# P7 of the last five output blocks as seven inner products, with a hand-written order of four engines, in a pooling-mixer kernel

## The chip, the cores and the metric

The kernel runs on one core of one Trainium2 chip. The metric is device microseconds of one execution; lower is better. The names used for the engines are those of the profile: PE is TensorE's matrix multiplication and PEld its weight load, DVE is VectorE, ACT is ScalarE, POOL is GpSimd, SP is SyncE, which only issues transfers.

## The reference

With DEPTH = 1 only mixer 0 of the model is used. It works on x of 4096 rows and 1024 columns, in f32:

```python
normed = rms_norm(x, norm_w)
u, gate = split(normed @ in_w, 2)                 # in_w: 1024 x 2048
for g, window in enumerate((2, 4, 8, 16)):        # four groups of 256 channels
    pooled = trailing_mean(u[g], window) - u[g]
    mixed[g] = pooled @ group_w[g] + group_b[g]
y = mixed * scale * silu(gate)
h = x + y @ out_w                                 # out_w: 1024 x 1024
out = rms_norm(h, final_norm_w)
```

rms_norm divides each row by the root of the mean of its squares (plus 1e-6) and multiplies by a weight for each column. trailing_mean takes the mean of the last 2, 4, 8 or 16 rows.

## The kernel before

**Arithmetic.** TensorE multiplies in a reduced format (fp32r), so each f32 operand is split into a high half and a low half: `split` (L177) has ACT copy the high half and DVE subtract it from the source to get the low one. Each product is three passes, high x high, high x low and low x high (`mm3`, L774). Around that lies Strassen's scheme in Winograd's form: a multiplication of two matrices, each cut into 2 x 2 quarters, is made as seven products P1 to P7 of sums of quarters, instead of eight.

**Stages.** The group maps are folded into in_w on the chip first. The input stage takes four blocks of 1024 tokens, each for two halves of the channels, and stores y to DRAM (`yd`). The output stage, which this case is about, takes eight blocks of 512 tokens (`NBO = 8`, b = 0 to 7 in the code). For each it makes `y @ out_w` as P1, P7, P6, P2, P5, P4, P3 in this order (`ORDER_OUT`), adds x, and normalizes and stores the rows.

**One block of the output stage.** Quarters "11", "21", "12" and "22" of y are loaded (`load_o`, L1068) and each product's left operand is formed on DVE and split (`split_o`, L1082) into one of four operand tiles. The sums of Winograd's scheme are S1 = 21 + 22, S2 = S1 - 11, S3 = 11 - 21 and S4 = 12 - S2; S1 is P5's operand, S2 is P6's, S3 is P7's and S4 is P3's. The right operands, the seven sums of out_w, lie split in `w[P1]` to `w[P7]`. A product (`product_out`, L894) is 24 matmuls of 128 x 512: two halves of the rows (j), four slices of the inner dimension (k), three passes. They accumulate in PSUM banks; each block has four pairs of banks, x (P1, P2), v (P7, P4), y (P6, P5, P3) and a spare, and the pairs rotate from block to block (`sets_of`, L1315). ACT copies P1's result from x to y, so that P6, P5 and P3 accumulate on it, as P2 does on x.

`evict_o` (L1214) takes the results out. In the first seven blocks P7, P6 and P2 are copied by ACT into the row tiles `hs`, and a transfer on POOL's queue adds x to them in place (`add_h`, L1059); P5, P4 and P3 are added to them by DVE. In the last block x is loaded first (`load_h`, L1048) and all six are added by DVE. After P4 the lower rows are complete, after P3 the upper ones; `finish` (L1116) then has ACT square them (a full row tile of 1024 into an SBUF tile, with the sum alongside), POOL and DVE work out the reciprocal root (`inverse`, `rsqrt`), DVE scale the rows, and SP's queue store them. The last block's rows are finished in halves (`early_half`, `late_factor` L1163, `late_scalar`, `late_vector`).

**Inner products that exist already.** From the third block on P2 is itself made by Winograd's scheme: `split_inner` (L847) forms the left operands from the four quarters of "12" and their sums, `form_inner` (L819) the right ones once, in the second block, into four tiles that are kept, and `product_inner` (L867) is one inner product, six matmuls of 128 x 256. P2's seven are spread: five in P2's place, P6 inside P5, and two groups' results added to rows by DVE (`add_inner`, L884). In the input stage `product_seven` (L713) does the same for P7 of two blocks, with copies from one PSUM cell to another on ACT.

**Order.** The program is written step by step (product by product), and each step says how far ahead it may load (four steps) and split (two steps): `advance`, L1538. The order of the instructions on each engine is that of a scheduler, which works from the dependences and from hints of the form "issue this after that" (`tc.issue_after`). In the output stage there are few such hints.

Of the kernel before, what the change touches and what calls it, by code (L numbers as in the profile page):

```python
# [10 lines left out]
F32 = mybir.dt.float32  # L11
# [16 lines left out]
NV = 8  # L28
EPS = 1e-6
# [6 lines left out]
class Slots:  # L36
# [21 lines left out]
    def give(self, ap):  # L58
        _, t = self.used.pop(id(ap))
        Slots.clock += 1  # L60
        self.free.append((Slots.clock, t))


@with_exitstack
def kernel(
# [35 lines left out]
    nc = tc.nc  # L101

# [62 lines left out]
    def add(dst, a, b):  # L165
        nc.vector.tensor_tensor(out=dst, in0=a, in1=b, op=ALU.add)

    def sub(dst, a, b):
        return nc.vector.tensor_tensor(out=dst, in0=a, in1=b, op=ALU.subtract)  # L169

    def mul(dst, a, b):
        nc.vector.tensor_tensor(out=dst, in0=a, in1=b, op=ALU.mult)  # L172

    def copy(dst, src, func=AF.Copy):
        return nc.scalar.activation(dst, src, func)  # L175
# [32 lines left out]
    nc.vector.memset(eps, EPS)  # L208
    scrap = const.tile([P, 1], F32, name="scrap")
    nc.scalar.activation(scrap, eps, AF.Sqrt)  # L210
# [3 lines left out]
    def rsqrt(dst, tmp, ms, ss, on_vector=False, first=False):  # L214

        root = nc.scalar.activation(tmp, ss, AF.Sqrt, bias=eps, scale=1.0 / D).ins
        (nc.vector if on_vector and not first else nc.gpsimd).tensor_scalar(
            out=ms, in0=ss, scalar1=1.0 / D, scalar2=EPS, op0=ALU.mult, op1=ALU.add
        )
        nc.vector.reciprocal(out=dst, in_=tmp)  # L220
        if on_vector:
            mul(tmp, dst, ms)
            mul(tmp, tmp, dst)
            nc.vector.tensor_scalar(
                out=tmp, in0=tmp, scalar1=-0.5, scalar2=1.5, op0=ALU.mult, op1=ALU.add
            )
            done = nc.vector.tensor_tensor(out=dst, in0=dst, in1=tmp, op=ALU.mult).ins
            roots.append((root, done))
            return
        nc.gpsimd.tensor_tensor(out=tmp, in0=dst, in1=ms, op=ALU.mult)  # L230
        nc.gpsimd.tensor_tensor(out=tmp, in0=tmp, in1=dst, op=ALU.mult)
        nc.gpsimd.tensor_scalar(
            out=tmp, in0=tmp, scalar1=-0.5, scalar2=1.5, op0=ALU.mult, op1=ALU.add
        )
        nc.gpsimd.tensor_tensor(out=dst, in0=dst, in1=tmp, op=ALU.mult)  # L235
# [3 lines left out]
    def load_rows(mat, k, c):  # L239
        u = take()  # L240
        nc.sync.dma_start(
# [4 lines left out]
    def copy_scaled(dst, u, c):  # L246
        done = nc.scalar.activation(dst[:, 0], u, AF.Copy, scale=c)
        nc.vector.scalar_tensor_tensor(
# [5 lines left out]
    def scale_rows(u, cs):  # L254
        for j in range(2):
            nc.scalar.activation(u[:, j], u[:, j], AF.Copy, scale=cs[j])  # L256
# [19 lines left out]
    def store_weights(dst, h, b11, b21, b12, b22):  # L276
        nc.sync.dma_start(out=dst[P1][h], in_=b11)
        nc.sync.dma_start(out=dst[P2][h], in_=b21)
        for i, u in combine(b11, b21, b12, b22).items():
            nc.sync.dma_start(out=dst[i][h], in_=u)  # L280
# [6 lines left out]
    def load_wb(i):  # L287
        for h in range(2):
# [5 lines left out]
            for name, place, used in (("t3", t3d[h], (P6, P7)), ("22", wvd[2 + h], (P5, P3))):  # L294
                if i in used:
                    p[name] = take()
                    nc.sync.dma_start(out=p[name], in_=place)

    def save_t3():

        for h in range(2):
            us = []
            for k in (h, 2 + h):
                us.append(take())
                nc.sync.dma_start(out=us[-1], in_=wvd[k])
            with tc.issue_after(evicted[0]):
                sub(us[0], us[1], us[0])
            nc.sync.dma_start(out=t3d[h], in_=us[0])
# [3 lines left out]
    def scaled(u, cs, other, op):  # L312

        for j in range(2):
            nc.vector.scalar_tensor_tensor(
# [42 lines left out]
    def load_w(src, i):  # L358
        for h in range(2):
            u = take()  # L360
            nc.sync.dma_start(out=u, in_=src[i][h])
# [18 lines left out]
    def load_group_w(q, halves=(0, 1), g=None):  # L380
        if g is None:
            g = take("p (t c) -> p t c", early, t=4)
        for j in halves:
            c = slice(2 * j, 2 * j + 2)
            nc.sync.dma_start(
# [4 lines left out]
    def load_wut(q, k, queues=(nc.sync,)):  # L390
# [16 lines left out]
    def fold(q, k, g, r, ps2, pool=None, on_vector=False, midway=None):  # L407
# [23 lines left out]
        for kk in range(2):  # L431
            if on_vector and kk == 0:
                with tc.issue_after(roots[0][1]):
                    nc.vector.tensor_scalar(
# [3 lines left out]
            else:  # L438
# [4 lines left out]
                nc.scalar.activation(dst, src, AF.Copy, scale=norm_c[k + kk])  # L443
# [6 lines left out]
    def load_row(b, half, j, pool=None):  # L450
# [3 lines left out]
        nc.sync.dma_start(out=u[:, 0], in_=rows[:, j, :])  # L454
        held[b, half, j] = u

    def square_row(b, half, j):
# [3 lines left out]
        done = nc.scalar.activation(  # L461
# [12 lines left out]
    def store_rs(b, half, rs):  # L474
        nc.gpsimd.dma_start(out=rd[b][half][0].rearrange("(p j) -> p j", j=4), in_=rs)
# [28 lines left out]
    def load_rstd(b, half):  # L504
        if half == 0:
            rstd[b] = take()
        nc.gpsimd.dma_start(out=rstd[b][:, half], in_=rd[b][half][0].partition_broadcast(P))
# [20 lines left out]
    def split_halves(us, saved=None):  # L528
        ts = []
        for h, u in enumerate(us):  # L530
            t = split_half(u)
            if saved is not None:
                first_saves.append(nc.gpsimd.dma_start(out=saved[h], in_=u).ins)
# [3 lines left out]
    def load_x(b, half, kh):  # L537
        us = []
        for h in range(2):
            u = take()  # L540
            k = 4 * kh + 2 * h
            nc.sync.dma_start(out=u, in_=xt[2 * b + 1 - half, :, k : k + 2, :])
# [3 lines left out]
    def load_saved(b, i):  # L546
        us = []
        for h in range(2):
            u = take()
            nc.sync.dma_start(out=u, in_=sd[b][i][h])  # L550
# [115 lines left out]
    def form_seven(stage):  # L666

        if stage == 0:
            seven["raw"] = [take() for _ in range(2)]
            for h, u in enumerate(seven["raw"]):  # L670
                nc.sync.dma_start(out=u, in_=t3d[h])
# [30 lines left out]
    def load_plain():  # L702
        seven["plain"] = take("p (n k c) -> p n k c", n=2, k=2)
        nc.sync.dma_start(out=seven["plain"][:, 0], in_=t3d[0][:, :, 0:256])
# [8 lines left out]
    def product_seven(t, v, middle, end):  # L713
# [46 lines left out]
        for c in range(2):  # L760
            bank = v[c].rearrange("p (j b) -> p j b", j=2)
            added = nc.vector.tensor_tensor(
# [937 lines left out]
```

## Time and profile before

| | |
|---|---|
| median of 3 runs | 909.38 us (908.97 to 909.73) |
| the profiled execution | 909.13 us, of which the span is 907.3 |
| granted TensorE clock, mean | 0.997 |
| PE, PEld busy | 898.9 us (99%), 790.2 us (87%) |
| DVE, ACT, POOL busy | 731.5 us (81%), 494.0 us (54%), 83.9 us (9%) |
| read and written | 117.81 MB and 60.83 MB, 197 GB/s |

The span is the stretch from the first to the last instruction that the profile shows. A row of the timeline gives the start within the span, the busy time, the engine, the line, the operation and its tiles, the shape, and how many instructions were put together; what stands in brackets is the idle time before it and what ended it. In a group, the last numbers are busy time, mean nanoseconds of one, and idle time. In a row of DMA issues the last number is the median time from issue to landing. Matmuls overlap, so their busy times are longer than the distance between their starts.

### The profile page before, as it was taken

To read this page: it belongs to the slowest core of one execution; us is meant where nothing else is said; L and a number is where in the kernel's file an instruction comes from. 1 tells how busy PE (TensorE), PEld (TensorE's weight loads), DVE (VectorE), ACT (ScalarE), POOL (GpSimd) and SP (SyncE) were. 2 spreads that over 40 slices of the span, in tenths; PEclk is the share of its full clock that TensorE was granted. 3 is DMA by queue.
4 is the path that set the end of the run, shared out by engine and by line. 5 is a ranking of instruction groups with operands and counts; after the bars stand their busy time and mean duration, and the time that the engine had idled before them with its cause. 6 is when DMAs were issued, how large, how long until landed. Compare 5 with 4: busy or idle time off the path is not lost.

```text
span 907.3 us, 11824 instructions
## 1 busy us (share of the span) xinstructions
PE 898.9 (99%) x4392; PEld 790.2 (87%) x4392; DVE 731.5 (81%) x868; ACT 494.0 (54%) x760; POOL 83.9 (9%) x166
## 2 busy tenths in 40 slices
PE   9999999999999999999999999999999999999996
PEld 7888888888888888889889888888888898988986
DVE  3889896985995999798599499599759768868686
ACT  7869547447446565346545636545535435445434
POOL 0020100100110000000000000001122113112200
PEclk9999999999999999999999999999999999999998
DMA  9987667677575462323554475528585675775732
GB/s 341 401 303 238 251 229 229 215 270 251 224 267 198 161 217 85 110 100 116 206 189 148 176 267 168 192 70 232 173 232 172 171 192 158 169 220 162 175 140 92
DMA packets 71401, 179.41 MB, mean 198 GB/s; under 512 B 6576, under 2 KB 24624, under 8 KB 71344
## 3 DMA queue, kind: packets, MB, share of 16 engines
q1 hardware_dynamic: 58720, 146.13, 46.4%
q0 software_dynamic: 11904, 31.48, 13.5%
q10 hardware_dynamic: 720, 1.06, 0.3%
q8 instruction: 34, 0.56, 0.3%
q14 instruction: 23, 0.19, 0.1%
HBM read 117.81 MB, written 60.83 MB: 197 GB/s over the span
## 4 chain that ended last, share of the span: by engine, by line
PE 95%; DVE 2%; DMA 1%; ACT 1%; issue 0%; DVEq 0%; ACTq 0%
PE bank L779 89%; PE bank L879 3%; PE bank L725 2%; PE bank L421 1%; DMA st<-in_x 1%; DMA early<-in_wut 0%; ACT st L461 0%; DVE vt L1245 0%; ACT st L1152 0%; PE bank L487 0%; DVE vt L172 0%; DVE w L169 0%; ACT st L443 0%; ACT early L443 0%; DVE vt L1204 0%
## 5 line engine op out<-in xcount | busy, mean ns | idle before, releaser
L779 PE MATMUL bank<-op,w 128*128 128x512 f32 x2592 | 560.9, 379 | 0.0
L779 PEld LDWEIGHTS bank<-op,w 128*128 128x128 f32 x2592 | 489.4, 189 | 70.2 <-ACT vt L175 0.4
L779 PE MATMUL bank<-w,op 128*128 128x512 f32 (+1 forms) x1212 | 262.2, 377 | 0.0
L779 PEld LDWEIGHTS bank<-w,op 128*128 128x128 f32 x1212 | 226.0, 189 | 31.0
L169 DVE TENSOR_TENSOR op<-st,op 128x1024 fp32r<-128x1024 f32 x134 | 162.3, 1219 | 58.0 <-ACT op L175 57.6
L175 ACT ACTIVATE op<-st 128x1024 fp32r<-128x1024 f32 x134 | 140.2, 1052 | 113.4 <-PE bank L779 64.5
L175 ACT ACTIVATE vt<-bank 128x512 f32<-128x512 f32 (+1 forms) x115 | 65.8, 590 | 46.5 <-PE bank L779 43.1
L169 DVE TENSOR_TENSOR st<-st,st 128x1024 f32<-128x1024 f32 (+1 forms) x42 | 45.8, 1104 | 18.9 <-ACT st L256 16.8
L169 DVE TENSOR_TENSOR op<-vt,op 128x1024 fp32r<-128x1024 f32 x42 | 51.1, 1219 | 8.1 <-ACT op L175 8.1
L175 ACT ACTIVATE op<-vt 128x1024 fp32r<-128x1024 f32 x42 | 44.1, 1054 | 24.9 <-PE bank L779 20.9
L1062 POOL DMA_DIRECT2D st<-in_x x19 | 16.8, 893 | 387.0 <-DVE op L169 352.9
L175 ACT ACTIVATE st<-bank 128x512 f32<-128x512 f32 (+1 forms) x61 | 34.7, 585 | 30.6 <-PE bank L779 19.1
L175 ACT ACTIVATE bank<-bank 128x512 f32<-128x512 f32 (+1 forms) x60 | 32.1, 537 | 30.1 <-PE bank L779 26.0
L933 DVE TENSOR_TENSOR_SCAN vt<-vt,window 128x1040 f32<-128x1040 f32 x16 | 37.9, 2376 | 1.6 <-DMA yd<-vt 1.5
L169 DVE TENSOR_TENSOR w<-st,w 128x1024 fp32r<-128x1024 f32 (+1 forms) x26 | 30.8, 1198 | 9.2 <-ACT w L175 9.2
L175 ACT ACTIVATE w<-st 128x1024 fp32r<-128x1024 f32 (+1 forms) x26 | 26.6, 1035 | 17.4 <-PE bank L779 9.5
L175 ACT ACTIVATE vt<-tails 128x32 f32<-128x32 f32 x28 | 6.3, 228 | 46.8 <-DVE vt L933 25.7
L979 DVE SCALAR_TENSOR_TENSOR vt<-vt,vt 128x1024 f32<-128x1024 f32 x24 | 29.3, 1219 | 0.3
L172 DVE TENSOR_TENSOR st<-st,vt 128x1024 f32<-128x1024 f32 x22 | 26.1, 1215 | 3.4 <-DMA vt<-rd 3.4
L1125 DVE SCALAR_TENSOR_TENSOR vt<-vt,ors,st 128x1024 f32<-128x1024 f32 x18 | 22.5, 1282 | 7.6 <-POOL ors L235 7.6
L1245 DVE TENSOR_TENSOR st<-bank,st 128x512 f32<-128x512 f32 x23 | 15.8, 689 | 14.0 <-PE bank L779 14.0
L984 DVE SCALAR_TENSOR_TENSOR st<-vt,colt,st 128x512 f32<-128x512 f32 x38 | 26.8, 743 | 0.1
(143 smaller groups left out, 735.3 us busy)
## 6 DMA issues: line engine op xcount, KB each, us to landing
st<-in_xt SPq DMA_DIRECT2D x28, 512.0 KB, 6.3
sd<-st POOLq DMA_DIRECT2D x28, 512.0 KB, 4.0
st<-sd SPq DMA_DIRECT2D x26, 512.0 KB, 4.2
st<-in_x SPq DMA_DIRECT2D x20, 512.0 KB, 6.0
st<-yd SPq DMA_DIRECT2D x20, 512.0 KB, 4.6
yd<-st SPq DMA_DIRECT2D x19, 512.0 KB, 3.1
out<-vt SPq DMA_DIRECT2D x18, 512.0 KB, 4.6
st<-wod SPq DMA_DIRECT2D x15, 512.0 KB, 4.0
```

The costliest lines, as they stand in the source:

```text
L169: return nc.vector.tensor_tensor(out=dst, in0=a, in1=b, op=ALU.subtract)
L172: nc.vector.tensor_tensor(out=dst, in0=a, in1=b, op=ALU.mult)
L175: return nc.scalar.activation(dst, src, func)
L725: latest[0] = nc.tensor.matmul(cell(n, c).rearrange("p (a s) -> p a s", s=2), x1, x2, start=i == P1 and k + m == 0, stop=k == 1 and m == 2 ...
L779: latest[0] = nc.tensor.matmul(ps, a, b, start=start and n == 0, stop=stop and n == 2, skip_group_check=True).ins
L879: latest[0] = nc.tensor.matmul(ps, x1, x2, start=i in (P1, P7) and k + n == 0, stop=k == 1 and n == 2, skip_group_check=True,).ins
L933: nc.vector.tensor_tensor_scan(out=sums_[:, HIST:], data0=flat[:, HIST:], data1=flat[:, HIST - win : 2 * end - win], initial=first_sum, op ...
L979: nc.vector.scalar_tensor_tensor(out=s[:, :, at : at + H], in0=s[:, :, at : at + H], scalar=1.0 / win, in1=v[:, :, HIST:], op0=ALU.mult, o ...
L984: nc.vector.scalar_tensor_tensor(out=sg[:, j], in0=s[:, j, at : at + H], scalar=bias_c[2 * grp + j], in1=sg[:, j], op0=ALU.add, op1=ALU.mult,)
L1062: nc.gpsimd.dma_start(out=hs[b][half, j][:, n], in_=x[row_of(b, half, j), n * H : (n + 1) * H], accum_op=ALU.add,)
L1125: nc.vector.scalar_tensor_tensor(out=us[j], in0=us[j], scalar=rs[:, j : j + 1], in1=fw[0], op0=ALU.mult, op1=ALU.mult,)
L1245: partial["added"] = nc.vector.tensor_tensor(out=dst, in0=src, in1=dst, op=ALU.add).ins
```

## The change

- **P7 by inner products.** In the last five blocks (`OWN = 3`: b = 3 to 7) P7 is made as seven inner products of six matmuls of 128 x 256: `own_first` has P1 and P5, `own_into` one product each. Four copies on ACT (`own_move`) carry a partial result from one cell of the v banks to another, one of them to SBUF, from where DVE adds it (`own_add`). The left operands are the quarters of S3 and four sums of them; the right ones are formed from out_w's P7 in the third block (`sum_inner`, `split_weight`).
- **The order by hand.** All calls to DVE, ACT, POOL and SP go through `InOrder`, which, while it is on, chains each instruction behind the one that was written before it for the same engine. It is switched on at the third block's P4 and off at the last block's P2. `steady` writes out every step from there on, and from the fourth block on it says for each product what is loaded, formed, split, evicted, squared and scaled beside it, and in which order. The inner products of P7 stand between the halves of P1's second row half and of P6.
- **S1 by transfers.** From the fourth block on the sum 21 + 22 is made by two transfers on POOL's queue that add "22" from DRAM to the loaded "21".
- **Rows.** Squares are taken of half rows, into PSUM banks that are free at the time, and the two sums are added on POOL (`square_rows`, `root`); `factor` and `norm_row` do what `finish` did. The finished rows of the first seven blocks are stored from POOL's queue instead of SP's.
- **Weights' places and P2's order.** P2's inner weights are formed in place in the loaded tiles, and kept in three tiles with one of P2's own weight tiles' quarters as the fourth home; P7's the same, and its two loaded tiles then serve as the temporary tiles for sums. The order of P2's inner products becomes P2, P4, P1, P3, P7, and in the third block the second half of `split_inner` comes a step later.

The core of the diff:

```diff
+class InOrder:
+    on = False
+    def __init__(self, tc, engine):
+        self.tc, self.engine, self.last = tc, engine, None
+    def __getattr__(self, name):
+        f = getattr(self.engine, name)
+        def call(*args, **kwargs):
+            behind = InOrder.on and self.last is not None
+            with self.tc.issue_after(self.last) if behind else nullcontext():
+                r = f(*args, **kwargs)
+            self.last = getattr(r, "ins", None)
+            return r
+        return call
...
+    def own_first(t, sets):
+        own.clear()
+        own.update(t=t, v=sets["v"])
+        own_into(P1, 1, True)
+        own_into(P5, 3)
+        own["m5"] = temp(1, "p (a b) -> p a b", a=4)[:, 0]
+        own_move(0, 1)
+        own_move(None, 3)
...
-            for p in (P2, P3, P4, P1, P7):
+            for p in (P2, P4, P1, P3, P7):
                 product_inner(p)
...
+    def square_rows(b, half, sets, j):
...
+        for n in range(2):
+            scalar.activation(
+                sets["v" if half else "y"][j], r["us"][j][:, n], AF.Square,
+                accum_out=r["parts"][:, n, j : j + 1],
+            )
...
+    def norm_row(b, half, j):
+        r = rows_of[b, half]
+        u = r["us"][j]
+        vector.scalar_tensor_tensor(
+            out=u, in0=u, scalar=r["rs"][:, j : j + 1], in1=fw[0], op0=ALU.mult, op1=ALU.mult
+        )
+        gpsimd.dma_start(
+            out=out[row_of(b, half, j), :], in_=u.rearrange("p a b -> p (a b)")
+        )
...
+    def steady(n):
+        _, b, i = steps[n]
+        sets, s, c = sets_of("o", b), oxs[b], b + 1
+        final, t = c == NBO, None
...
+        if i == P1:
...
+            out_part(P1, t, sets["x"][0], 0, range(4))
+            square_rows(b - 1, 0, past, 0)
+            copy(sets["y"][0], sets["x"][0])
+            factor(b - 1, 1)
+            sub(s["11"], s["21"], s["11"])
+            ready[P6] = next_op("p (s a b) -> p s a b", **whole)
+            split(ready[P6], s["11"])
+            with tc.issue_after(latest[0]):
+                out_part(P1, t, sets["x"][1], 1, range(2))
+            own_first(ready.pop(P7), sets)
+            with tc.issue_after(latest[0]):
+                out_part(P1, t, sets["x"][1], 1, range(2, 4))
+            copy(sets["y"][1], sets["x"][1])
+            square_rows(b - 1, 0, past, 1)
+            for j in range(2):
+                norm_row(b - 1, 1, j)
+        elif i == P7:
...
+            own_into(P2, 0)
+            own_into(P6, 1)
+            own_move(2, 1)
...
+            split(both, s["12"])
+            root(b - 1, 0)
+            with tc.issue_after(latest[0]):
+                out_part(P6, ready[P6], sets["y"][0], 0, range(2))
+            own_into(P7, 2)
+            own_into(P3, 1)
+            own_move(3, 2)
+            with tc.issue_after(latest[0]):
+                out_part(P6, ready[P6], sets["y"][0], 0, range(2, 4))
+            own_into(P4, 2)
+            factor(b - 1, 0)
+            norm_row(b - 1, 0, 0)
+            own_add()
...
+        elif i == P6:
...
+            high(sums_op, v)
+            norm_row(b - 1, 0, 1)
+            low(sums_op, v)
...
+            evict_o(b, P7, sets)
...
+            split(ready[P5], s["21"])
+            with tc.issue_after(latest[0]):
+                out_part(P6, ready.pop(P6), sets["y"][1], 1, range(4))
+            evict_o(b, P6, sets)
+        elif i == P2:
...
+            split(ready[P4], s["22"])
+            InOrder.on = not final
+            product_out(P2, ready.pop(P2), sets, False)
+            evict_o(b, P2, sets)
+        elif i == P5:
+            sub(s["12"], s["12"], s["11"])
+            ready[P3] = next_op("p (s a b) -> p s a b", **whole)
+            split(ready[P3], s["12"])
+            product_out(P5, ready.pop(P5), sets, False)
+            evict_o(b, P5, sets)
+        elif i == P4:
+            if not final:
+                ahead["12"] = load_y(c, 0, 1)
+                ready[P1] = next_op("p (s a b) -> p s a b", **whole)
+                split(ready[P1], ahead["11"])
+                u = temp(0, "p (a b) -> p a b", a=4)
+                sub(u, ahead["11"], ahead["21"])
+                for k in range(0, 4, 2):
+                    gpsimd.dma_start(
+                        out=ahead["21"][:, k : k + 2], in_=yd[c][:, 4 + k : 6 + k, 0:TH],
+                        accum_op=ALU.add,
+                    )
+                ready["own"] = op_halves()
+                high(ready["own"][1], u)
+            product_out(P4, ready.pop(P4), sets, False)
+            evict_o(b, P4, sets)
+        else:
+            if not final:
...
+                square_rows(b, 1, sets, 0)
...
+                high(sums_op, v)
+                square_rows(b, 1, sets, 1)
+                root(b, 1)
+                plain_op, both = ready.pop("own")
+                low(both, u)
+                low(sums_op, v)
...
+            product_out(P3, ready.pop(P3), sets, final)
+            evict_o(b, P3, sets)
```

More of the change, by code (lines that the diff above doesn't have):

```diff
@@ L28 @@
 NV = 8
+OWN = 3
 EPS = 1e-6
@@ L101 @@
     nc = tc.nc
+    InOrder.on = False
+    vector, scalar, gpsimd, sync = (
+        InOrder(tc, e) for e in (nc.vector, nc.scalar, nc.gpsimd, nc.sync)
+    )
     const = ctx.enter_context(tc.tile_pool(name="const", bufs=1))
@@ L867, in product_inner, with own_add @@
+    def own_add():
+        bank = own["v"][1].rearrange("p (j b) -> p j b", j=2)
+        add(bank, bank, own["m5"].unsqueeze(1).to_broadcast([P, 2, 256]))
     def product_inner(i):
-        t, sets = inner["t"], inner["sets"]
+        sets = inner["sets"]
         bank, half = {
```

496 lines of the change are left out of this document (317 added, 179 removed).

## The prediction

> **What bounds the kernel now.** I read the page first: the busy times and the chain that ended last.
>
> ```profile
> span 907.3 us, 11824 instructions
> PE 898.9 (99%) x4392; PEld 790.2 (87%) x4392; DVE 731.5 (81%) x868; ACT 494.0 (54%) x760; POOL 83.9 (9%) x166
> PE 95%; DVE 2%; DMA 1%; ACT 1%; issue 0%; DVEq 0%; ACTq 0%
> ```
>
> TensorE (PE) is busy from end to end and is 95% of the chain. Its ends are modelled, so I read starts too: first its waits, then its timeline in the fifth output block (I count the eight blocks from 1; the code's b is one less), then the last entry of that timeline.
>
> ```profile
> PE bank L1374 <- PEq L1685: 0.8, 1, 0.8
> PE bank L421 <- DMA early<-in_group_w: 0.4, 1, 0.4
> ...
> 775.91 2.75 PE L779 MATMUL bank<-w,op 128*128 128x512 f32 x12
> 778.50 0.83 PE L879 MATMUL bank<-inner,op 128*128 128x256 f32 x6
> 779.17 2.75 PE L779 MATMUL bank<-w,op 128*128 128x512 f32 x12
> ...
> 889.74 10.61 PE L779 MATMUL bank<-w,op 128*128 128x512 f32 x60
> ```
>
> Both waits are in the first microseconds. Start to start, twelve long matmuls take 778.50 - 775.91 = 2.59, so 0.216 each, and six short ones 779.17 - 778.50 = 0.67, so 0.112 each. Nothing lies between them: in the output stage PE already runs at its pitch. The last matmul ends at 900.35, and 6.95 us of tail follow. So the time can fall only by issuing less on PE, and rises by every wait that the new order gives PE. The margin of the other engines is in the windows (columns: window, width, then PE, PEld, DVE, ACT, POOL busy, granted clock, DMA share, GB/s):
>
> ```profile
> 775.00:800.00 25.00, 25.00 (x128) 22.18 (x127) 19.04 (x28) 12.06 (x19) 3.87 (x9) 1.00 0.64 169
> ```
>
> The vector engine (DVE) has 24% left, the scalar engine (ACT) half. The clock is full, so no term comes from it.
>
> **P7 as seven inner products.** A block's P7 is 24 long matmuls, 24 x 0.216 = 5.18 us. It becomes 7 x 6 = 42 short ones, 42 x 0.112 = 4.70. That removes 0.48 a block and 2.40 in five blocks, all on the path. A block from the fourth on is then 120 long and 84 short ones: 35.3 us for 35.8.
>
> The Trainium skill, "TensorE: Matmul & The Clock Gate", section "Back-to-back issue gap", gives a sustained spacing of 81 ns for 128 columns and 131 ns for 512, weight loads included. Between them 256 columns would be an estimated 98 ns, and P7 would go from 3.1 to 4.1 us: the change would lose about 1 us a block. The trace's 216 and 112 ns differ from that, and stand.
>
> **The moves between inner products.** Four copies by ACT inside PSUM carry partial results, and PE waits for three of them. The nearest rows are the same scheme in the input stage:
>
> ```profile
> 422.74 1.62 PE L725 MATMUL bank<-op,inner 128*128 128x256 f32 x12
> 424.19 1.61 PE L725 MATMUL bank<-op,w 128*128 128x256 f32 x12
> ...
> 423.00 0.37 ACT L175 ACTIVATE bank<-bank 128x256 f32<-128x256 f32 x1
> ```
>
> Twelve short ones took 1.45 instead of 1.34: PE waited 0.1 for that move. The new order puts long matmuls of P1 and P6 in between, which covers two of the three. The third is late by its place on ACT. I need pitches of ACT and DVE:
>
> ```profile
> 426.81 2.05 ACT L175 ACTIVATE vt<-bank 128x512 f32<-128x512 f32 x4
> 891.41 0.63 ACT L1152 ACTIVATE st<-vt 128x512 f32<-128x512 f32 x1
> 892.17 0.63 ACT L1152 ACTIVATE st<-st 128x512 f32<-128x512 f32 x1
> 710.20 2.01 ACT L175 ACTIVATE op<-st 128x1024 fp32r<-128x1024 f32 x2 [5.36 <-PE bank L779]
> 778.70 0.69 DVE L1245 TENSOR_TENSOR st<-bank,st 128x512 f32<-128x512 f32 x1 [1.06 <-PE bank L779]
> 711.76 2.35 DVE L169 TENSOR_TENSOR op<-st,op 128x1024 fp32r<-128x1024 f32 x2
> 882.09 1.28 DVE L1245 TENSOR_TENSOR vt<-bank,vt 128x512 f32<-128x512 f32 x2
> 800.88 0.16 DVE L220 RECIPROCAL ors<-otmp 128x2 f32<-128x2 f32 x1
> 802.24 2.48 DVE L1125 SCALAR_TENSOR_TENSOR vt<-vt,ors,st 128x1024 f32<-128x1024 f32 x2 [1.21 <-POOL ors L235]
> ```
>
> Pitches: eviction on ACT 0.49, squares of a half row 0.76 (892.17 - 891.41), a high half on ACT 0.96; a full DVE operation 1.13, a DVE add from PSUM 0.60, a row scaling 1.20. DVE starts 0.20 after PE's last matmul of a product gives way (778.70 against 778.50). From a reciprocal to the scaling that needs it through GpSimd (POOL) are 1.36.
>
> Let T be time from a block's first P1 matmul. PE has P1 behind it at 18 x 0.216 + two products of 0.67 + 6 x 0.216 = 6.53. ACT evicts it from 6.73, squares two half rows (1.52), then moves: 7.22 + 1.52 + 0.37 = 9.11. PE wants that cell at 6.53 + 1.34 + 1.30 = 9.17, less than a hand-over away. I take 0.1 a block (bounds 0 and 0.2), 0.5 in all.
>
> **DVE's written order in blocks 4 to 7.** Counted: twelve full operations (13.6), four scalings (4.8), six PSUM adds (3.6), the rest some 6: 28 of 35.3 us, about the share of before. What matters is its order. The scalar half of the P2 rows runs on ACT 9.0 to 10.1, DVE's low half to 11.3, then a reciprocal, 1.36 through POOL, a scaling (to 13.8), the inner sum's add (14.4), a scaling (15.6), the low half of the inner sums (ends 16.9). PE wants that at 15.07 + 3 x 0.67 + 0.22 = 17.3, as 15.07 ends P1, P7 and P6. It holds by 0.4, the tightest place; the next, P5's low half, by 0.7. Cost 0.
>
> **S1 by transfers.** One DVE add (1.13) leaves, and with it nothing on the path. Two accumulating DMAs on POOL's queue come, behind DVE's subtraction, which ends near T = 29.4:
>
> ```profile
> L1062 POOL DMA_DIRECT2D vt<-in_x x22 | 19.4, 929 | 57.8 <-DVE vt L889 32.1 <-ACT vt L175 16.6 <-ACT op L175 8.3
> vt<-in_x POOLq DMA_DIRECT2D x20, 256.0 KB, 5.3
> ...
> sd<-st POOLq DMA_DIRECT2D x28, 512.0 KB, 4.0
> sd<-vt POOLq DMA_DIRECT2D x4, 512.0 KB, 5.8
> ```
>
> Issue 0.93, landing 5.3: the sum is there at 35.7, T = 0.4 of the next block, where DVE asks at 0.9. ACT is busy with P1's eviction until 3.3, so up to 1.5 late is free. Cost 0; two microseconds later still, 0.2 a block.
>
> **Blocks 1 to 3, and the weights.** PE's order there is the same but for two leaves of P2. P7's inner weights are eight half-size DVE operations in block 3, 8 x 0.60 = 4.8 us once, beside DVE's idle quarter; without that cover up to 1. I take 0. Rows' final stores move from SP to POOL (weighed under the rivals). The tail's instructions are the same: 6.95.
>
> **The last block.** Here P7, P6 and P2 are evicted by DVE adds, not by ACT, and stand in the same DVE order. P5's first matmul accumulates on the bank of P6, so it waits for P6's first add, in front of which the built order has: scaling, inner add, scaling, low half of the sums, both adds of P7, low half of P5. And a subtraction (S4) now stands between the reciprocal and the scaling, while POOL works on the factor:
>
> ```profile
> 764.64 1.22 DVE L169 TENSOR_TENSOR vt<-vt,st 128x1024 f32<-128x1024 f32 x1
> 764.78 1.13 POOL L217 TENSOR_SCALAR oms<-oss 128x2 f32<-128x2 f32 x1 [8.04 <-ACT st L1121]
> 798.84 0.19 POOL L217 TENSOR_SCALAR oms<-oss 128x2 f32<-128x2 f32 x1 [6.91 <-ACT st L1121]
> ...
> 766.37 1.23 DVE L169 TENSOR_TENSOR op<-st,op 128x1024 fp32r<-128x1024 f32 x1 [0.43 <-ACT op L175]
> 766.37 1.28 POOL L231 TENSOR_TENSOR otmp<-otmp,ors 128x2 f32<-128x2 f32 x1
> ```
>
> A POOL operation that meets a full DVE operation on SBUF takes 1.13 instead of 0.19: it ends when DVE's does. So POOL's chain stands until the subtraction's end (11.3 + 1.22 = 12.5) and then needs its 0.9: the scaling starts at 13.4, not 12.6. From there 1.20 + 0.60 + 1.20 + 1.13 + 2 x 0.60 + 1.13 = 6.5, then P6's add of 0.69 and a hand-over of 0.15: 20.7. PE stands there at 15.07 + 5 x 0.67 (inner products of P2) + 2 x 0.216 (two matmuls of P4 that the order has there) + the 0.1 = 18.95. PE waits 1.8 us. If the subtraction does not hold POOL, 12.6 leads to 19.9 and a wait of 0.95. I take 1.8, as each overlap I found with a full DVE operation under way held POOL.
>
> **Sum.** -2.40 + 0.5 + 1.8 = -0.1 on the profiled execution's 909.13, which is 0.25 under the median of the runs. On the median: 909.38 - 0.1 = 909.3.
>
> **The rivals.** I call a difference within 0.2% (1.8 us) no change, about what these runs can tell apart.
>
> *The wait in the last block does not come* (an earlier add, or PE's order leaving enough to do in front of P5). For it: PE waited nowhere in the output stage before. Against: the adds above are queued on one engine and each has a row. Then -2.40 + 0.5 = -1.9, 907.5. Chance 0.17.
>
> *The stores become the wait.* A row scaled on DVE is now stored from POOL's queue, and ACT's eviction of P2 goes into the same tile. The scaling ends at 13.9 and 15.7; with the 4.0 of a POOL store the tiles are free at 17.9 and 19.7, and ACT gets there at 18.2. With 5.8 they are free at 19.7 and 21.5. Behind the second stand ACT's eviction and high half for P3, DVE's low half, and the add that PE's last inner product of P2 needs at 24.3: 21.5 + 0.59 + 1.06 + 1.22 + 0.42 + hand-overs = 25.0, so 0.7 or 0.8 a block in four blocks. It decides from landings over 5.2 us. For it: SP's stores of such rows land in 4.8 at the median,
>
> ```profile
> out<-vt SPq DMA_DIRECT2D x17, 512.0 KB, 4.8
> ```
>
> and six more accumulations share the queue. Against: the next block's loads are fired from T = 18 on, behind these stores, so the stores fly nearly alone. Then -0.1 + 4 x 0.75 = +2.9, 912.2. Chance 0.18.
>
> *The weight load sets the pitch of short matmuls.* A load takes 192 ns, more than their 112:
>
> ```profile
> L879 PEld LDWEIGHTS bank<-w,op 128*128 128x128 f32 x108 | 13.5, 192 | 0.3
> ```
>
> If it were not hidden, 42 x 0.192 = 8.06 for 5.18, +2.9 a block, 923.7. Six in 0.67 us, from this very group, speak against it. Chance 0.01; the skill's spacing above is counted here too.
>
> *The change is not in the program*: the built order shows the 84 short matmuls a block and DVE's order as told, so I give it nothing.
>
> The forecast has the remaining 0.64, its own range 908.3 (POOL not held) to 910.6 (0.2 a block for the moves, 0.2 for S1, or some wait for the new weights).
>
> **How the numbers follow.** Faster by over 0.2% is the first rival and a little of the forecast's edge: 0.18. Slower is the second and third: 0.2. No change: 0.62. The range reaches from the first rival with the moves at their lower bound, 909.38 - 2.40 = 907.0, to the second, 912.2.
>
> **What would show it.** After: 420 short matmuls in the place of 120 long ones gone from the five last blocks; block starts 35.3 to 35.4 apart. In the last block a gap of 1 to 2 us in PE's starts ahead of P5, ended by a DVE add; a POOL operation near 1.1 us beside the subtraction. Gaps ahead of P2's last inner products in blocks 4 to 7 would speak for the stores. The prediction is wrong if the last block has no gap, or if any earlier block has one over 0.3.

## The result: 2.7% slower, and the profile after

The changed kernel takes 934.1 us at the median (933.36 to 935.05, 4 runs), the kernel before 909.56 in the same comparison (908.97 to 910.36). The ratio is 1.027, with a 95% interval of 1.0252 to 1.0288. The forecast was 909.3 in a range of 907.0 to 912.2, and slower by over 0.2% had a chance of 0.2. The profiled execution took 935.05, of which the span is 933.3.

The page of after, parts 1 and 4:

```profile
span 933.3 us, 12155 instructions
PE 904.8 (97%) x4482; PEld 796.3 (85%) x4482; DVE 745.8 (80%) x903; ACT 514.2 (55%) x847; POOL 113.7 (12%) x218
PE 86%; DVE 4%; issue 3%; DMA 3%; ACT 2%; POOL 1%; SPq 0%; DVEq 0%; ACTq 0%; POOLq 0%
```

PE falls from 95% to 86% of the chain, and every other name in it gets a share. The count of matmuls, 4482 for 4392, is the one expected: 210 short ones more, 120 long ones fewer. (The prediction's 420 are all short ones of the five blocks, those of P2 included.) All calls of the wrapped engines now carry line 79, that of `InOrder`, so the rows below are told apart by their tiles. PE's waits in after (what waited, what ended it, us in total, times, longest):

```profile
PE bank L947 <- ACT bank L79: 17.3, 5, 4.1
PE bank L805 <- DVE st L79: 1.1, 1, 1.1
```

L947 is an inner product, and "ACT bank" is a move of a partial result from one PSUM cell to another: five waits, one a block, in the five blocks of the change. The second row is the wait that was forecast for the last block. From the distances between the starts of matmuls, the difference of the two spans (26.0) is made up like this:

| term | us |
|---|---|
| fewer and shorter matmuls, as forecast | -2.4 |
| PE waits in the fourth block, 2.8 and 0.8 | +3.5 |
| PE waits ahead of the third inner product of P7, blocks 5 to 8: 4.2, 3.2, 4.2, 3.7 | +15.3 |
| PE wait ahead of P5 in the last block | +1.3 |
| matmuls at half rate after these waits | +7.2 |
| start of the run (the first main matmul at 33.60 instead of 32.70) and the tail | +1.0 |

The chain of waits of after, in order of time, over the start of the fifth block (start, us, what):

```profile
758.33 0.81 issue
759.14 1.22 POOL st L79
760.36 4.12 issue
764.48 4.66 DMA st<-yd
769.14 0.03 issue
...
769.23 1.24 DVE st L79
770.47 0.02 issue
770.49 0.03 ACT op L79
770.52 0.93 issue
771.45 0.38 ACT bank L79
771.83 0.04 issue
771.87 2.93 PE bank L947 x12
```

Read upwards from PE: the inner products wait for the move on ACT (771.45); ACT has the high half of S2 in front of it (770.49); that waits for S2 itself, DVE's subtraction (769.23); and that waits for S1, whose second transfer lands at 769.14. Above it stands the line that matters: 4.12 us of "issue", in which POOL waits for nothing that the profile shows, between S1's first transfer and its second. POOL's timeline in after:

```profile
752.04 0.85 POOL L79 DMA_DIRECT2D vt<-in_x  x1 [2.49 <-ACT op L79]
753.14 0.85 POOL L79 DMA_DIRECT2D vt<-in_x  x1 [0.25 <-issue]
759.14 1.22 POOL L79 DMA_DIRECT2D st<-yd  x1 [5.14 <-DVE vt L79]
764.48 1.21 POOL L79 DMA_DIRECT2D st<-yd  x1 [4.12 <-issue]
765.23 0.68 POOL L79 TENSOR_TENSOR oss<-parts 128x2 f32<-128x2 f32 x1
```

With the landings beside these rows the pattern shows. The x accumulation of 752.04 lands at 758.81, and S1's first transfer starts 0.33 later; that one lands at 764.14, and the second starts 0.34 later. In all five blocks S1's second transfer starts 0.33 to 0.34 us after the first has landed, and its first starts 0.33 after an x accumulation has landed. DVE, which the row at 759.14 names as the releaser, had ended its subtraction at 755.2.

The clock (windows of after: window, width, busy times, granted clock, DMA share, GB/s):

```profile
765.00:770.00 5.00, 2.83 (x19) 2.29 (x18) 0.94 (x2) 2.11 (x6) 1.87 (x7) 1.00 0.37 52
770.00:775.00 5.00, 3.13 (x13) 3.06 (x14) 3.88 (x4) 3.64 (x9) 0.64 (x1) 0.67 0.00 0
```

After the wait of 4.2 us the granted clock is 0.67 in the next window, and short matmuls start every 0.213 us instead of 0.112, long ones every 0.427 instead of 0.216, until 775.3. After the waits of 3.2 to 4.2 us in the other three blocks the granted clock is 0.66 over five microseconds as well; after the waits of 0.8, 1.3 and 2.8 us it stays at 1.00.

The Trainium skill, "TensorE: Matmul & The Clock Gate", section "Part 1: The HAM clock gate (the "warmup" mystery)", has the array's clock halved after an idle window of about 3.4 us, until it has been busy for about as long. The stretches after the waits of 3.7 and 4.2 us agree with the rule; that after the wait of 3.2 us, a little shorter than such a window, does so only roughly.

### The profile page after: what moved, and what is told of

It reads as the page before. It is cut to its first block, busy times and chain, and to the rows that moved or that the text cites. A ratio compares the mean times of both kernels' runs of the same rounds, so it can differ in the third digit from the quotient of the medians.

```text
span 933.3 us, 12155 instructions
## 1 busy us (share of the span) xinstructions
PE 904.8 (97%) x4482; PEld 796.3 (85%) x4482; DVE 745.8 (80%) x903; ACT 514.2 (55%) x847; POOL 113.7 (12%) x218
## 4 chain that ended last, share of the span: by engine, by line
PE 86%; DVE 4%; issue 3%; DMA 3%; ACT 2%; POOL 1%; SPq 0%; DVEq 0%; ACTq 0%; POOLq 0%
PE bank L805 79%; PE bank L947 5%; DVE vt L79 2%; PE bank L751 2%; DMA st<-yd 1%; DMA vt<-yd 1%; DVE op L79 1%; DMA early<-in_wut 1%; ACT st L79 1%; PE bank L447 1%; DVE st L79 0%; POOL st L79 0%; ACT w L79 0%; POOL vt L79 0%; ACT op L79 0%
## 5 line engine op out<-in xcount | busy, mean ns | idle before, releaser
L805 PE MATMUL bank<-w,op 128*128 128x512 f32 (+1 forms) x1092 | 242.8, 380 | 1.1 <-DVE st L79 1.1
L805 PEld LDWEIGHTS bank<-w,op 128*128 128x128 f32 x1092 | 204.3, 192 | 28.9 <-DVE st L79 1.5
L79 POOL DMA_DIRECT2D vt<-in_x x39 | 34.3, 999 | 401.7 <-DVE vt L79 352.9
L79 DVE TENSOR_TENSOR st<-st,st 128x1024 f32<-128x1024 f32 (+1 forms) x56 | 66.2, 1200 | 20.2 <-ACT st L79 16.8
L79 DVE TENSOR_TENSOR op<-vt,op 128x1024 fp32r<-128x1024 f32 x54 | 65.6, 1220 | 12.2 <-ACT op L79 11.9
L79 DVE TENSOR_TENSOR vt<-bank,vt 128x512 f32<-128x512 f32 (+1 forms) x117 | 66.4, 595 | 11.1 <-PE bank L805 6.2
L947 PE MATMUL bank<-w,op 128*128 128x256 f32 x264 | 37.1, 284 | 17.9 <-ACT bank L79 17.3
L947 PEld LDWEIGHTS bank<-w,op 128*128 128x128 f32 x264 | 34.8, 196 | 21.3 <-ACT bank L79 19.3
L79 ACT ACTIVATE st<-st 128x1024 f32<-128x1024 f32 x33 | 34.8, 1056 | 23.1 <-DVE st L79 20.0
L79 DVE TENSOR_TENSOR st<-st,vt 128x1024 f32<-128x1024 f32 (+1 forms) x35 | 40.3, 1171 | 1.6 <-DMA vt<-rd 1.6
L79 DVE TENSOR_TENSOR vt<-vt 128x1024 f32<-128x1024 f32 (+3 forms) x41 | 37.7, 921 | 0.2
```

The lines of the kernel that those rows point to most:

```text
L79: r = f(*args, **kwargs)
L805: latest[0] = nc.tensor.matmul(ps, a, b, start=start and n == 0, stop=stop and n == 2, skip_group_check=True).ins
L947: latest[0] = nc.tensor.matmul(ps, x1, x2, start=start and k + n == 0, stop=k == 1 and n == 2, skip_group_check=True,).ins
```

## The experiments

Theory (rows): POOL's queue has room for a limited number of rows of transfers in flight, at least 384 and fewer than 512. An x accumulation, a store and each of S1's transfers have 128, 128 and 256. (The traces bear this count out for the accumulating transfers, but not for the stores: see the last section.) Rivals: the stretch is too full of transfers (bunching); accumulations into one tile, or bytes in flight, are what is limited; or the moves' place in ACT's order makes the wait.

**S1 on DVE.**

```diff
             factor(b - 1, 1)
+            add(s["21"], s["21"], s["22"])
             sub(s["11"], s["21"], s["11"])
...
-                for k in range(0, 4, 2):
-                    gpsimd.dma_start(out=ahead["21"][:, k : k + 2], in_=yd[c][...], accum_op=ALU.add)
```

> The changed kernel with S1 made by one DVE addition in front of S2's, instead of two transfers. Theory (rows): POOL's queue has room for a limited number of rows, from 384 to 511 of them; so S1's first transfer waits for one of x to land and the second for the first, S1 comes some 9 us late, and PE waits 3 to 4.5 us a block and then runs at half rate. Without the transfers the waits go: 934.1 - 18.9 - 7.2 = 908, range 907 to 911, with the last block's wait of 1.3 still there. Rival (bunching): the hand-written order puts a block's loads, its x accumulations and its stores into one stretch in which the DMA engines are full; then quarter 22 comes late as well, and the time stays above 920.

Measured: 908.44 us (908.19 to 909.99, 10 runs) against 909.8 for the kernel before; ratio 0.9988, interval 0.9978 to 0.9997. The whole loss is gone, and this version is a little faster than both kernels. Its page, PE's waits in the output stage, and the same stretch of the chain:

```profile
span 906.5 us, 12123 instructions
```

```profile
PE bank L805 <- DVE st L79: 1.1, 1, 1.1
PE bank L947 <- DVE op L79: 0.2, 1, 0.2
```

```profile
757.94 2.37 PE bank L805 x11
760.32 1.34 PE bank L947 x12
761.65 1.30 PE bank L805 x6
762.95 1.34 PE bank L947 x12
```

PE passes from P1 into the inner products and on without a gap. Bunching falls: the same loads, stores and x accumulations stand in the same stretch (y loads take 11.5 us and more at the median here too), and PE waits for none of them.

**Half of S1 on DVE.** One transfer of 256 rows is left, and DVE adds the other half.

```diff
+            add(s["21"][:, 2:4], s["21"][:, 2:4], s["22"][:, 2:4])
             sub(s["11"], s["21"], s["11"])
...
-                for k in range(0, 4, 2):
+                gpsimd.dma_start(out=ahead["21"][:, 0:2], in_=yd[c][:, 4:6, 0:TH], accum_op=ALU.add)
```

> The changed kernel with only the first of S1's two transfers; the other half is added by DVE (0.6 us). Theory (rows): the first still waits for room until about the block's start and lands some 4.5 us after it; what is saved is the second's 4.7 us, about the whole of PE's wait: 908 to 912. Rival (bunching): above 920. If the first transfer's own wait were enough to hold PE, a wait of 0.5 to 1.5 us a block would stay: 912 to 917.

Measured: 910.35 us (909.09 to 912.04, 10 runs), ratio 1.0006 (0.9996 to 1.0015). The remaining transfers land in 4.2 to 5.3 us. So it is the second that costs nearly all. This version is still 1.9 us slower than the one with all of S1 on DVE, with PE waits of 0.4 to 1.0 in the last two blocks.

**Four transfers of 128 rows.** The same bytes into the same tile.

```diff
-                for k in range(0, 4, 2):
+                for k in range(4):
-                        out=ahead["21"][:, k : k + 2], in_=yd[c][:, 4 + k : 6 + k, 0:TH],
+                        out=ahead["21"][:, k : k + 1], in_=yd[c][:, 4 + k : 5 + k, 0:TH],
```

> The changed kernel with S1's sum as four transfers of 128 rows (one slice each) instead of two of 256 rows; same bytes, same queue. Theory (rows): a transfer of 128 rows finds room where one of 256 does not, so the first goes some 4 us earlier and three are in flight at once; the last lands some 3.5 to 4.5 us earlier than now, PE's wait falls from 4 to under 1 us a block: 908 to 916. Rival (one tile): two accumulations into one tile go one after the other whatever their size; then four take 4 x 4.5 us instead of 2 x 4.7, PE's wait grows by some 8 us a block: above 960. Rival (moves): unchanged, 934, as S1's landing is not what PE waits for.

Measured: 918.34 us (917.7 to 920.56, 4 runs), ratio 1.0098 (1.0083 to 1.0114): two thirds of the loss gone, and 2 us above the expected range. POOL's timeline:

```profile
743.63 0.87 POOL L79 DMA_DIRECT2D vt<-in_x  x1 [3.26 <-ACT op L79]
747.20 1.75 POOL L79 DMA_DIRECT2D vt<-in_x  x2 [2.70 <-ACT op L79]
750.96 0.88 POOL L79 DMA_DIRECT2D st<-yd  x1 [2.00 <-DVE vt L79]
754.06 0.88 POOL L79 DMA_DIRECT2D st<-yd  x1 [2.22 <-issue]
755.79 0.88 POOL L79 DMA_DIRECT2D st<-yd  x1 [0.85 <-issue]
757.22 0.87 POOL L79 DMA_DIRECT2D st<-yd  x1 [0.56 <-issue]
```

The landings here are 750.65, 753.75 and 755.49 for the three x accumulations and 756.92 for S1's first: each S1 transfer starts 0.31 after one of these. Three of 128 rows fly at a time and the fourth waits for the oldest. So accumulations into one tile are not serialized (that rival said 960 and more). Four issues of 0.88 and waits for room still bring S1 in late, at 760.68.

**Half the rows, the same bytes.** S1's two transfers read 128 rows of 2 KB. These are other columns of y, so the sum that is made is not S1.

```diff
-                        out=ahead["21"][:, k : k + 2], in_=yd[c][:, 4 + k : 6 + k, 0:TH],
-                        accum_op=ALU.add,
+                        out=ahead["21"][:, k : k + 2].rearrange("p a b -> p (a b)"),
+                        in_=yd[c][:, 4 + k // 2], accum_op=ALU.add,
```

> The changed kernel with S1's two transfers reading other columns of y: 128 rows of 2 KB each instead of 256 rows of 1 KB, so the same bytes and the same number of transfers in half the rows (what is added is not quarter 22, so the output differs from the reference's). Theory (rows): two transfers of x and S1's first are 384 rows and fit, so S1's first is issued right behind DVE's subtraction, some 4 us earlier than in the changed kernel, and its second does not wait for the first but for one of x; S1 lands 5 to 8 us earlier and PE's wait of 3 to 4.5 us a block goes: 908 to 913. Rival (bytes or transfers in flight): nothing changes, 931 to 936.

Measured: 915.17 us (914.34 to 915.19, 4 runs), ratio 1.0062 (1.0047 to 1.0077). POOL's timeline:

```profile
751.27 0.87 POOL L79 DMA_DIRECT2D st<-yd  x1 [1.77 <-DVE vt L79]
754.90 0.87 POOL L79 DMA_DIRECT2D st<-yd  x1 [2.77 <-issue]
```

The second now starts 3.0 us before the first lands (757.93); it starts 0.31 after an x accumulation has landed (754.60). Neither the number of transfers nor their bytes changed against the changed kernel, only the number of rows (and with it their length), and 19 of the 25 us are back. The saving falls short of what was expected by 2 us: with three in flight these transfers take 5.5 to 7.7 us to land, S1 is there at 760.64, and waits of 0.5 to 1.6 us stay in the last four blocks.

**The moves ahead of S2 on ACT.**

```diff
-            split(ready[P6], s["11"])
             with tc.issue_after(latest[0]):
                 out_part(P1, t, sets["x"][1], 1, range(2))
             own_first(ready.pop(P7), sets)
+            split(ready[P6], s["11"])
```

> The changed kernel with ACT's order changed in one place: the two moves between P7's inner products stand ahead of the high half of S2 instead of behind it. Theory (rows): the moves are then in time, but PE has only twelve short matmuls (1.3 us) until it needs S2 for P6; the wait moves there and is shorter by 1.3 us a block, with some of the half rate gone: 922 to 930. Rival (moves): the place of the moves on ACT is the whole of the wait, and it goes: 908 to 911.

Measured: 933.19 us (931.45 to 933.89, 4 runs), ratio 1.0253 (1.0236 to 1.027), outside both expectations. PE's waits:

```profile
PE bank L805 <- ACT op L79: 5.6, 5, 1.4
PE bank L947 <- ACT bank L79: 5.0, 8, 1.0
PE bank L947 <- DVE op L79: 3.2, 4, 1.5
PE bank L805 <- DVE op L79: 2.8, 5, 0.6
```

The long wait broke up into short ones at other places, as long in sum (21.0 us for 20.1), with about half the half-rate time (4.0 us for 7.2), and the blocks stayed long: 39.8 to 40.4 us from one start to the next in blocks 5 to 8, for 40.3 to 41.3 in the changed kernel. What I had missed is that the late S1 is a ring, not a single wait. In after the first x accumulation of P2's rows starts at 752.04; 7.1 later S1's first transfer starts, 5.3 later its second, which lands in 4.7; 2.7 more bring PE into P7's third inner product, and 21.3 us of PE's work lead to the next block's x accumulation at 793.19. That is 41.1, a block's length. By this reading, which is of one block and was not tested by itself, taking a wait away on PE shortens the ring only by what PE can do meanwhile.

**P7 as 24 long matmuls again**, on the version with S1 on DVE.

```diff
-            own_first(ready.pop(P7), sets)
...
-            own_into(P2, 0)
-            own_into(P6, 1)
-            own_move(2, 1)
+            product_out(P7, ready.pop(P7), sets, False)
```

> The kernel of s1_dve with P7 of the last five blocks as 24 long matmuls again (its inner weights, sums, moves and the addition left out, the rest of the hand-written order kept). By the pitches, 0.216 and 0.112 us, the seven inner products are worth 0.48 us a block, 2.40 in five: 908.4 + 2.4 = 910.8, and 0.3 less where an engine has it easier: 910.3 to 911. Rival (nothing gained): the moves and DVE's extra work eat it, 908.4 or less.

Measured: 910.64 us (910.34 to 911.62, 11 runs), ratio 1.0015 (1.0006 to 1.0024). The two ratios are 0.0027 apart, 2.5 us, with some 1.2 either way by their intervals; from the first main matmul to the last matmul's end the two profiled executions are 2.2 apart. The inner products bring what the pitches say, as expected.

**S4 behind the scalings in the last block**, on the same version.

```diff
-            sub(s["12"], s["12"], s["11"])
+            with tc.issue_after(rows_last[0]):
+                sub(s["12"], s["12"], s["11"])
```

> The kernel of s1_dve with S4's subtraction in the last block behind the two row scalings on DVE, instead of between the reciprocal and the first scaling. The step of the prediction: the subtraction holds POOL's first operation of the factor until its own end, which costs 0.9 of PE's wait of 1.28 in front of P5. Then the wait falls to about 0.4 and the time to 907.5, if the tail's order stays worth the same. Rival: POOL's row is long for another reason, the wait stays, 908.4.

Measured: 908.48 us (908.11 to 909.48, 11 runs), ratio 0.9989 (0.998 to 0.9998): no gain where 0.9 us was expected. DVE and POOL in the last block with S1 on DVE:

```profile
873.21 0.16 DVE L79 RECIPROCAL ors<-otmp 128x2 f32<-128x2 f32 x1
873.33 1.22 DVE L79 TENSOR_TENSOR vt<-vt,vt 128x1024 f32<-128x1024 f32 x1
875.47 1.28 DVE L79 SCALAR_TENSOR_TENSOR vt<-vt,ors,st 128x1024 f32<-128x1024 f32 x1 [0.92 <-POOL ors L79]
873.52 1.08 POOL L79 TENSOR_TENSOR otmp<-ors,oms 128x2 f32<-128x2 f32 x1 [1.69 <-DVE ors L79]
```

The same with S4 moved as well:

```profile
874.22 0.16 DVE L79 RECIPROCAL ors<-otmp 128x2 f32<-128x2 f32 x1
875.60 1.28 DVE L79 SCALAR_TENSOR_TENSOR vt<-vt,ors,st 128x1024 f32<-128x1024 f32 x1 [1.22 <-POOL ors L79]
874.53 0.20 POOL L79 TENSOR_TENSOR otmp<-ors,oms 128x2 f32<-128x2 f32 x1 [1.69 <-DVE ors L79]
```

The mechanism is there: POOL's operation takes 1.08 beside the subtraction and 0.20 without it, and from the reciprocal to the scaling are 1.38 instead of 2.26. But PE's order changed with it: the two matmuls of P4 that stood ahead of P5 (0.43) now stand behind, so PE arrives earlier and waits 1.2 as before. From the first main matmul to the last matmul's end the gain is 0.29.

**P7's additions behind P6's as well.**

```diff
+            if not final:
+                evict_o(b, P7, sets)
...
             evict_o(b, P6, sets)
+            if final:
+                evict_o(b, P7, sets)
```

> As s4_after, and in the last block P7's two additions on DVE stand behind P6's instead of ahead of them. PE's wait in front of P5 hangs on P6's first addition alone and should be gone: 907.1 (range 906.6 to 907.8), by the two causes named in the prediction for the last block. Rival: P4 accumulates on P7's bank and comes to wait for the later additions, or DVE has less time in the tail; then 908 or more.

Measured: 908.76 us (908.33 to 909.59, 11 runs), ratio 0.9993 (0.9985 to 1.0002). This is above the expected range. The wait ahead of P5 is gone, and 0.9 us of it comes back 4 us later, ahead of an inner product of P2 that waits for DVE. In both orders that were tried PE comes to wait for DVE in this stretch.

**The hand-written order off**, with S1 on DVE.

```diff
-            InOrder.on = n == own_from - 2 or InOrder.on
+            InOrder.on = False
```

> The kernel of s1_dve with the chains between instructions off: the same work, its order on DVE, ACT, POOL and SP left to the scheduler, as before the change. Theory (rows): the loss lay in S1's transfers, not in the order; the scheduler's order had no gap on PE before, so about 908 to 912. Rival (order): seven inner products leave too little room for an order that is not written out; gaps of 1 us and more in several blocks, 913 or more.

Measured: 940.38 us (936.9 to 941.54, 4 runs), ratio 1.0333 (1.0315 to 1.0351). The theory's number was wrong here. PE's waits, and the row of DVE behind the longest:

```profile
PE bank L947 <- DVE vt L79: 19.1, 4, 5.8
```

```profile
752.98 1.22 DVE L79 TENSOR_TENSOR st<-st,st 128x1024 f32<-128x1024 f32 x1 [7.20 <-DMA st<-yd]
```

The scheduler put a full DVE operation that needs a y load ahead of work that PE needs, and DVE stood 7.2 us until the load landed. So the order by hand is no part of the loss; in this program it is what avoids another of the same size. Whether the inner products are what leaves the scheduler's order too little room, as the rival has it, is not shown: there is no run without them and without the order.

**S1 by transfers alone**, in the kernel before.

```diff
-            add(s["21"], s["21"], s["22"])
+            if b < 3: add(s["21"], s["21"], s["22"])
+            else: # the two accumulating transfers of the change
```

> The kernel before with S1 of the last five blocks made by the same two transfers of 256 rows instead of the DVE addition, and nothing else; the scheduler orders the rest. Theory (rows): the second transfer again starts when the first has landed, so S1 takes some 10 us from the first issue; but here PE makes P7 between P1 and P6, 5 us more of cover, and the subtraction that follows is not chained ahead of other work. A small loss, 0 to 1 us a block: 909 to 914. Rival (the transfers always cost PE the block's 4 us): 925 or more.

Measured: 913.14 us (911.74 to 915.92, 5 runs), ratio 1.0048 (1.003 to 1.0067). The pairs again start one after the other, for instance

```profile
852.83 1.22 POOL L1095 DMA_DIRECT2D vt<-yd  x1 [10.24 <-DVE st L169]
859.67 1.22 POOL L1095 DMA_DIRECT2D vt<-yd  x1 [4.66 <-issue]
```

where the first lands at 859.33. The order there has slack for it in most blocks; PE waits once for long in the output stage, 2.9 us.

## Why the prediction was wrong

**The step that failed** is "S1 by transfers ... Cost 0". It took each transfer's price from fitting rows (issue 0.93, landing 5.3; S1's transfers took 1.2 and 4.1 to 5.0) and laid them side by side: both issued when DVE's subtraction is done, both landed 5.3 later, "the sum is there at 35.7, T = 0.4 of the next block". The subtraction ended where the step has it. But the first transfer then stood 4 us for room, and the second 5.3 for the first, and S1 was there 8.0 us after the block's first matmul. The term put at 0 cost 18.9 us of waits and, with the half rate behind them, 26 us. Landing times measure a transfer once it is issued, and say nothing of how many are let in. The size was wrong as well: "0.2 a block" for two microseconds of lateness takes a late S1 as something that PE's cover absorbs; with every engine in a written order it came back in the next block.

**The trace of before showed the limit.** Of four x accumulations that POOL issues in a row, the fourth starts late (POOL's timeline of before):

```profile
768.62 1.81 POOL L1062 DMA_DIRECT2D st<-in_x  x2 [0.41 <-ACT op L175]
771.17 0.86 POOL L1062 DMA_DIRECT2D st<-in_x  x1 [0.74 <-ACT st L175]
775.69 0.88 POOL L1062 DMA_DIRECT2D st<-in_x  x1 [3.66 <-ACT vt L175]
```

The eviction that the fourth adds to ended at 774.09; the first of the four lands at 775.38, and the fourth starts 0.31 later. This row alone could be read otherwise, as an ACT operation ends at 775.37 too. The x accumulation at 668.84 cannot: it starts 0.69 after the last end on ACT, and 0.31 after an earlier one has landed (668.53). I read these rows for their lengths and not for the time between them.

**The half rate** was in no step: 7.2 us, included above. "The clock is full, so no term comes from it" held as long as PE did not stop.

**The other steps**, in the version with S1 on DVE, where they can be read alone:
- The inner products: 2.40 forecast, 2.2 to 2.5 measured. The blocks are 35.28 us apart, four times over (forecast 35.3 to 35.4). So the estimate worked out from the spacing that the Trainium skill gives ("TensorE: Matmul & The Clock Gate", section "Back-to-back issue gap"), by which the change would lose about 1 us a block, does not hold here; the measurement stands.
- The moves: 0.5 forecast, no wait in blocks 4 to 7.
- DVE's written order in blocks 4 to 7: cost 0 forecast, 0 found, with DVE's addition of S1 in it.
- The last block: 1.8 forecast, 1.3 measured, at the place named, ended by P6's first addition, with POOL held by S4's subtraction (1.08, and 1.09 in after). Without S1's transfers the forecast's sum would have been 0.9 us off in the time (908.44 for 909.3) and 1.3 in the change (909.8 to 908.44, where -0.1 was forecast): it had the moves and this wait too dear. Its lower value, for POOL not held, is a slip of 0.1: 909.38 - 2.40 + 0.5 + 0.95 is 908.4.

**The rivals.** The stores on POOL's queue took 3.0 us to land at the median, where that rival needed 5.2 (two of 22 took 5.4), and PE waited for none:

```profile
out<-vt POOLq DMA_DIRECT2D x22, 512.0 KB, 3.0
```

It looked at the right queue for the wrong transfers: it weighed how long they fly, and not how many rows POOL lets fly at once. The others did not come: the weight load stayed hidden, the change does what it says, and the wait in the last block was there.

## What to carry to other kernels

Before a transfer is counted as hidden, look in the trace for what else its queue has in flight, and whether the next issue there ever stood until an earlier one had landed: an idle stretch that ends as "issue", or at an engine that had long been done, just behind a landing is that sign. Count such a queue in rows as well as in bytes, and accumulating transfers apart from plain ones. Here, where the engines follow a written order, one late result was paid in every block, and moving the wait hardly shortened the ring; such a result is priced by going once around, from it to the next block's same step.

## What the runs showed of the hardware

- POOL's queue let at most 384 rows of accumulating transfers fly in each of the twelve traces (three of 128, or one of 256 with one of 128). At 512 the next issue waited, mostly until 0.31 to 0.34 us past an earlier landing, with no semaphore to show for it.
- Plain stores are not counted like that. In each trace seven of 128 rows of 4 KB flew at once early on, 896 rows; in after the seventh starts at 57.15, and the oldest then in flight lands at 58.30. In the output stage two stores flew beside two accumulations, and one beside three. In three runs, though, an accumulation that would have been the third beside two stores stood until a store had landed, in the one with 24 long matmuls until 0.31 past 739.86:

```profile
57.15 0.53 POOL L79 DMA_DIRECT2D sd<-st  x1
...
740.16 0.88 POOL L79 DMA_DIRECT2D vt<-in_x  x1 [1.57 <-issue]
```

If an accumulating row is counted twice and a plain one once, all twelve traces fit one limit: 896 were let in, and these issues stood where they would have made 1024. No run was made to test that. Where between these numbers the limit lies, and what sets it, stays open.

- A wait of PE over 3 us cost more than its length: the clock was half for 3.4 us, and in after 20.1 us of waits brought 7.2 more. Shorter waits mostly cost nothing more, but in the run with the moves first the clock was 0.66 over five microseconds once, in the sixth block, behind waits of 0.6, 1.2 and 0.7 us within 5 us; no idle window of 3.4 us stands there, so the rule cited above does not give it, and the measurement decides.
- The half-clock stretches lie on a grid. In after they start at 771.73, 812.69, 853.65 and 894.61, 40.96 apart each time, while the blocks are 40.3 to 41.3 long; with the order off they are 3.41 or 6.83 long and start 44.4, 41.0 and 44.4 apart, which are 13, 12 and 13 times 3.41. So it may depend on where a wait near 3 us falls whether half the clock follows; that was not tested.
